# State-space turns dealt at 0.8 per attention step for the first ten, at 1.25 afterwards

## The chip, the cores and the metric

The kernel runs on one core of one Trainium2 chip. What counts is the time on the device, in microseconds (us), as a median of several runs. One execution is recorded by the hardware profiler; its numbers are in the profile.

## The reference

One inference step of a one-layer trunk of width 1024. A prompt of 1024 rows and 8 running streams of 16 new rows each (128 "sample" rows, with 1024 cached rows per stream) go through the same layer. Three mixers work on the normalised input, one projection merges them, then cross-attention into 256 memory rows and a SwiGLU block follow:

```python
proj = einsum('bnd,de->bne', u, p['w_in'])                  # one projection feeds all three
sq, sk, sv, fq, fk, fv, fg, z, xbc, dt = split_last(proj, IN_SIZES)
sb_o  = sb_attend(...)                                      # stick-breaking attention, 4 heads of 64
fox_o = fox_attend(...)                                     # attention with a forget gate, 4 heads of 64
y, h_final = ssd_scan(xs * dt[..., None], dt * A, Bm, Cm, h0, ssd_chunk)   # state space, 8 heads of 64, state 128
y = y + p['d_skip'][:, None] * xs
ssd_o = rmsnorm(y * silu(z), p['ssd_norm_g'])
h = h + einsum('bne,ed->bnd', concatenate([sb_o, fox_o, ssd_o], -1), p['w_out'])
h = h + cross_attend(rmsnorm(h, g_x), mk, mv, wq_x, wo_x)
h = h + swiglu(rmsnorm(h, g_ffn), w_gate, w_up, w_down)
```

The new keys, values, forget gates, and the state-space states after the step (`p_ssm`, `s_ssm`) are outputs too.

## The kernel before, in words

**Engines.** TensorE (PE) multiplies and transposes, VectorE (DVE) and ScalarE (ACT) work on its results, GpSimd (POOL) does elementwise work, and SyncE (SP) issues the DMAs from one queue. Each takes its instructions in the order that was fixed when the program was built. A scheduler makes that order: it is given the instructions in the order of the Python code, and follows a plan of its own of when each would be ready. So the order of the code decides much, but not all.

**Attention steps.** `pipeline` yields once per row block and once per weighted sum, over 16 prompt units and 4 sample units for each of the two attention kinds, 112 steps in all. It is the outer loop of the stretch that matters here.

**Turns.** After each step the loop at L1328 adds a rate to `acc`, and for every whole turn in `acc` it lets the generator `fill` go on by one yield. `fill_all` first runs `dense` (`fill_s`, the remaining parts of the first projection, 68 turns) and then `ssd` (`ssd_gen`, 51 turns). `RATE[0]` holds while `dense` runs, `RATE[1]` afterwards. What is left of `fill` when the attention steps are over is woven into the output projection by `weave(fill, ho, WV, "ho")` behind the loop. `hp` has no entry for these turns and changes nothing.

**State-space turns.** `ssd_gen` first sets up the decays, then goes through nine blocks in the order 8, 0, 1, ..., 7. Block 8 is the 128 sample rows, blocks 0 to 7 are 128 prompt rows each. For each block:
- `load` fetches a tile A with three DMAs: L1055 from `xbcsc`, L1057 from `acsc`, L1059 from `zsc`. These tiles, the tiles B and two tiles `st8` with the decode states come from one pool of large tiles (`act` in the rows).
- `prepare` transposes A on PE (L1072, L1076); ACT copies the results into B (L1073, L1077).
- `weights` makes the decays: PE L1087, ACT L1095 and L1100 on A, DVE L1097, L1103.
- `states` for blocks 0 to 7 is two small groups of matmuls (L1112, L1118). For block 8 it updates the states of eight streams: PE transposes L1147, ACT copies L1149, PE L1150 and L1157, DVE L1162, and at the end of each half one DMA of the new states, L1164, `s_ssm<-act`. There are two of them, and each frees one `st8` tile when it has landed.
- `outputs` is PE L1174, DVE L1176, ACT L1179, DVE L1181; `write` is PE L1186, ACT L1187 and the DMA L1188 to `mixsc`.

**Others in the rows.** L573, L574, L576 are score matmuls of the prompt, L591 to L617 its weighted sums, L900 to L908 load and transpose cached keys, L942, L943 and L951 are the sample rows' weighted sums (transposes on PE, their copies on ACT, the sums on PE). `add_rows` (L1352, residual adds on DVE) and `load_rows` (L1402 to L1416) belong to the output projection; L341 to L343 are its matmuls.

Of the kernel before, what the change touches and what calls it, by code (L numbers as in the profile page):

```python
# [51 lines left out]
XS, XH = 1, 2  # L52
X0, X1, XL = 2, 2, 2
REV = ()
RATE = (1.0, 1.1, 60)
C_SQ, C_SK, C_SV, C_FQ, C_FK, C_FV, C_Z, C_XBC, C_DT = 0, 256, 512, 768, 1024, 1280, 1540, 2052, 3076


# [5 lines left out]
def tile_hybrid_step(ctx: ExitStack, tc: tile.TileContext, a: dict):  # L64
# [307 lines left out]
    def hp(k):  # L372
        return tc.high_priority(HP[k]) if HP.get(k) else nullcontext()
# [268 lines left out]
    def pipeline(units, lag, units1, lag1):  # L642

        prev = []
        for rows, av in units + units1:
            if (rows, av) == units1[0]:
                lag = lag1
            w = []
            for f in rows:
                with hp("row"):  # L650
                    w.append(f())
                yield
            prev.append((av, w))
            if len(prev) > lag:
                f, w = prev.pop(0)
                with hp("av"):
                    f(w)
                yield
        for f, w in prev:
            with hp("av"):  # L660
                f(w)
            yield
# [590 lines left out]
    def fill_s():  # L1253
        yield from dense_T(w_in, uc, [(C_FQ, consume_qk(4, 0, QS))])
        yield from dense_T(w_in, uc, [(C_FQ + P, consume_qk(5, 1, QS))])
        yield from dense_T(w_in, uc, [(C_FK, consume_qk(6, 0, None, p_k[1], s_k[1]))])
        yield from dense_T(w_in, uc, [(C_FK + P, consume_qk(7, 1, None, p_k[1], s_k[1]))])
        for n, _ in enumerate(proj_v(1, C_FV, p_v[1], s_v[1], extra=4)):
            if n == 6:
                head = w_unit(z_srcs(0), 0, 4)  # L1260
            yield
        zs, sums = z_proj(0, head), fox_sums()
        for _ in range(4):
            next(sums)
            yield
            next(zs)
            yield
        sct = load_pads()
        for n, _ in enumerate(zs):
            if n == 2:  # L1270
                pad_cols(sct)
            yield
        for o in ORD:
            if o == "z1":

                for hd in range(4):
                    tc.keep_in_program_order(
                        SP.dma_start(out=fs4.rearrange("(b h) i k -> b h i k", h=4)[:, hd],
                                     in_=fs_sc[hd].unsqueeze(1).to_broadcast([DEC_B, 4, PAST])))
                for p in range(4):  # L1280
                    tc.keep_in_program_order(
                        SP.dma_start(out=fqs[:, p:p + 1], in_=fn_sc[8 * p:8 * p + 8, :]))
            if o[0] == "z":
                yield from z_proj(int(o[1]))
            elif o == "dt":
                dt_softplus()
                yield
            else:
                yield from xbc_proj(*o)

    def mixed(m, at, fc, nxt):


        heads = [prompt_units(m, h, fc) for h in range(4)]
        loads = [load for _, load in heads[1:]] + [nxt]
        out = []
        for h, (units, _) in enumerate(heads):
            for i, (rows, av) in enumerate(units):
                if i == 3 and loads[h]:
                    rows = [lambda f=rows[0], load=loads[h]: (load(), f())[1]] + rows[1:]  # L1300
                out.append((rows, av))
        for i, u in reversed(list(enumerate(decode_units(m)))):
            out.insert(at[i], u)
        return out, heads[0][1]
# [10 lines left out]
    u0, _ = mixed(0, AT0, None, load1)  # L1315

    dense = fill_s()
    ssd = ssd_gen()
    done = [False]

    def fill_all():
        yield from dense
        done[0] = True
        yield from ssd

    fill = fill_all()
    acc = 0.0
    for k, _ in enumerate(pipeline(u0, LAG0, u1, LAG1)):  # L1328
        acc += RATE[1] if done[0] else RATE[0]
        while acc >= 1.0:  # L1330
            with hp("ssd" if done[0] else "dense"):
                next(fill, None)
            acc -= 1.0

# [743 lines left out]
    for c in range(NCH):  # L2078
        acc = [[banks[(6 * c + 2 * i + j) % 8]() for j in range(2)] for i in range(3)]
# [63 lines left out]
```

## Time and profile before

| | us |
|---|---|
| Runs | 1865.41, 1867.77, 1865.81 |
| Median | 1865.81 |
| Profiled execution, whole | 1868.44 |
| Its span | 1866.7 |
| PE busy | 1809.8 (97%) |
| DVE, ACT, POOL busy | 897.2, 796.8, 618.6 |
| Mean granted clock of PE | 0.988 of full |

The span runs from the first to the last instruction of the profiled execution; 1.7 us lie around it. PE is the fullest engine. A gap between two of its instructions has a releaser: the instruction or DMA that ended last before PE went on. "Granted clock" is the speed at which PE was let run, 1.00 or 0.50 in the stretch that matters; PE counts as busy at half clock too.

### The profile page before, as it was taken

Reading aid. Unit: us, or ns where it says so; the run is one execution under the profiler, and the core shown is the slowest. Engines: PE = TensorE matmul, PEld = TensorE weight load, DVE = VectorE, ACT = ScalarE, POOL = GpSimd, SP = SyncE. Lnnn points to the kernel's source line nnn. Section 1 sums busy time; section 2 is a strip of 40 time slices with the busy share of each in tenths; the row PEclk is TensorE's granted clock in tenths of the full one; section 3 lists DMA queues with packets and bytes.
Section 4 is the critical chain, followed back from the end, with each engine's and each line's share of the span. In section 5 each row is a group of like instructions: output and inputs, shape, how many; then the busy total and the mean of one; then the engine's idle time right before and its main releaser. Section 6 shows DMA issues by size and latency. Waiting matters only on the chain.

```text
span 1866.7 us, 32065 instructions
## 1 busy us (share of the span) xinstructions
PE 1809.8 (97%) x12008; PEld 1620.3 (87%) x12008; DVE 897.2 (48%) x1792; ACT 796.8 (43%) x1697; POOL 618.6 (33%) x921
## 2 busy tenths in 40 slices
PE   7999999999999999999999989999999999999998
PEld 5899788888967777899988889999999999888886
DVE  3412324465646874454553695333333334455554
ACT  6532544535446772343342464333333333344443
POOL 7622434525215663121021107444444542000000
PEclk9999999999988999999999989999999999999999
DMA  9465654527577883356873124332222223656572
GB/s 338 153 186 150 211 153 132 171 79 209 179 222 253 279 278 125 118 136 155 188 252 111 68 87 116 94 79 71 72 71 71 71 71 94 217 186 238 185 242 92
DMA packets 305548, 289.55 MB, mean 155 GB/s; under 512 B 113004, under 2 KB 257364, under 8 KB 305392
## 3 DMA queue, kind: packets, MB, share of 16 engines
q1 hardware_dynamic: 305392, 287.49, 51.0%
q8 instruction: 95, 1.56, 0.4%
q14 instruction: 61, 0.50, 0.1%
HBM read 221.58 MB, written 66.38 MB: 154 GB/s over the span
## 4 chain that ended last, share of the span: by engine, by line
PE 83%; DMA 7%; DVE 4%; POOL 2%; ACT 1%; issue 1%; SPq 0%; DVEq 0%; POOLq 0%; ACTq 0%
PE psd L1936 11%; PE psd L343 10%; PE psd L341 10%; PE psd L342 10%; PE pst L1936 8%; PE pss L341 4%; PE pss L343 4%; PE pss L342 4%; PE pss L1936 4%; PE pso L1936 2%; PE pst L343 2%; PE pst L342 2%; PE pst L341 2%; PE pso L606 2%; PE pst L591 1%
## 5 line engine op out<-in xcount | busy, mean ns | idle before, releaser
L341 PE MATMUL psd<-act,wh 128*128 128x384 f32 x528 | 183.0, 347 | 1.6 <-ACT xc L761 1.6
L343 PE MATMUL psd<-act,wl 128*128 128x384 f32 x528 | 180.7, 343 | 0.7 <-POOL wl L133 0.7
L133 POOL TENSOR_TENSOR wl<-wr,wh 128x256 fp32r<-128x256 f32 (+2 forms) x152 | 117.7, 809 | 192.0 <-ACT wh L295 185.2
L342 PE MATMUL psd<-act,wh 128*128 128x384 f32 x528 | 180.3, 342 | 0.0
L1936 PE MATMUL pst<-bT,tr 128*128 128x256 f32 (+1 forms) x1068 | 154.7, 292 | 0.0
L1936 PEld LDWEIGHTS pst<-bT,tr 128*128 128x128 f32 x1068 | 144.6, 188 | 0.1
L341 PE MATMUL psd<-wh,act 128*128 128x256 f32 (+3 forms) x414 | 131.6, 322 | 3.6 <-ACT act L1415 1.5
L343 PE MATMUL psd<-wh,act 128*128 128x512 f32 (+3 forms) x424 | 135.0, 320 | 0.0
L342 PE MATMUL psd<-wl,act 128*128 128x256 f32 (+3 forms) x414 | 132.5, 321 | 2.4 <-POOL wl L133 2.3
L1936 PE MATMUL psd<-bT,tr 128*128 128x320 f32 (+1 forms) x912 | 132.6, 294 | 0.7 <-POOL tr L133 0.7
L1936 PEld LDWEIGHTS psd<-bT,tr 128*128 128x128 f32 x912 | 124.5, 188 | 1.0 <-POOL tr L133 1.0
L133 POOL TENSOR_TENSOR tr<-u,tr 128x256 fp32r<-128x256 f32 x110 | 82.8, 780 | 100.6 <-ACT tr L1772 82.8
L133 POOL TENSOR_TENSOR ws<-ws 128x256 f32<-128x256 f32 (+2 forms) x100 | 72.8, 757 | 111.5 <-DVE ws L535 91.4
L256 POOL TENSOR_SCALAR sm<-sm 128x1 f32<-128x1 f32 (+2 forms) x27 | 9.3, 343 | 295.0 <-ACT y L2047 206.6
L1911 DVE TENSOR_TENSOR tr<-tr,pst 128x256 f32<-128x256 f32 (+1 forms) x86 | 38.6, 449 | 139.3 <-ACT tr L1908 106.2
L341 PEld LDWEIGHTS psd<-act,wh 128*128 128x128 f32 x528 | 99.9, 189 | 3.6 <-ACT xc L761 2.0
L343 PEld LDWEIGHTS psd<-act,wl 128*128 128x128 f32 x528 | 99.8, 189 | 3.2 <-issue 1.9
L342 PEld LDWEIGHTS psd<-act,wh 128*128 128x128 f32 x528 | 100.0, 189 | 2.9 <-issue 2.6
L133 POOL TENSOR_TENSOR tr<-raw,tr 128x256 fp32r<-128x256 f32 x94 | 69.4, 765 | 83.4 <-ACT tr L1772 75.3
L1772 ACT CAST tr<-u 128x512 fp32r<-128x512 f32 x130 | 76.5, 620 | 27.9 <-PE pst L1936 5.9
L341 PEld LDWEIGHTS psd<-wh,act 128*128 128x128 f32 x414 | 78.3, 189 | 10.6 <-issue 1.9
L342 PEld LDWEIGHTS psd<-wl,act 128*128 128x128 f32 x414 | 78.1, 189 | 10.4 <-POOL wl L133 4.2
(645 smaller groups left out, 4645.9 us busy)
## 6 DMA issues: line engine op xcount, KB each, us to landing
u<-w_down SPq DMA_DIRECT2D x40, 512.0 KB, 3.3
raw<-w_down SPq DMA_DIRECT2D x26, 512.0 KB
st<-qksc SPq DMA_DIRECT2D x48, 256.0 KB, 5.2
wr<-w_in SPq DMA_DIRECT2D x44, 256.0 KB, 3.2
tr<-hidsc SPq DMA_DIRECT2D x55, 192.0 KB, 3.3
hidsc<-tr SPq DMA_DIRECT2D x34, 288.0 KB
qksc<-sg SPq DMA_DIRECT2D x48, 192.0 KB, 2.9
wr<-cache_sb_k SPq DMA_DIRECT2D x32, 256.0 KB, 3.0
```

Of the source, the lines that this page charges most:

```text
L133: POOL.tensor_tensor(out=out[:, a0:a1], in0=in0[:, a0:a1], in1=in1[:, a0:a1], op=op)
L256: POOL.tensor_scalar(v, ss, inv, EPS, ALU.mult, ALU.add)
L341: PE.matmul(out, ah, bh, start=start, stop=False)
L342: PE.matmul(out, ah, bl, start=False, stop=False)
L343: PE.matmul(out, al, bh, start=False, stop=stop)
L591: PE.transpose(tp[:, o:o + P], w[:, (2 * kp + j) * P:(2 * kp + j + 1) * P], ident)
L606: return PE.matmul(po[r:r + 64, q_], vt[:, 2 * (k0 + i) + j, :], pfs[i][:, sl], start=start and k0 == 0 and (j == 0 or qp > 0), stop=k0 + ...
L1772: ACT.copy(hi, src)
L1911: DVE.tensor_tensor(out=at(out, g), in0=at(x, g), in1=ps[g][:, :GW[g]], op=op)
L1936: PE.matmul(dst[g][:, :GW[g]], x[:, ka], y[:, k, :], start=start and k == 0 and m == 0, stop=stop and k == 3 and m == 2, skip_group_check= ...
```

## The change

A rate of 0.8 holds for the first ten yields of `ssd_gen`, then 1.25 to the end of the attention steps. Before, it was 1.1 throughout. 44 attention steps remain when `dense` is through, so about 48 of the 51 turns were dealt before and about 49 are now; the rest goes to `weave`. The same instructions are issued, and on every engine the order is the same up to the first state-space blocks and again from the output projection on. Between them, PE instructions 3250 to 4055 of the program stand in another order.

```diff
--- before.py
+++ after.py
@@ -52,7 +52,7 @@
 XS, XH = 1, 2
 X0, X1, XL = 2, 2, 2
 REV = ()
-RATE = (1.0, 1.1, 60)
+RATE = (1.0, 0.8, 1.25)
 C_SQ, C_SK, C_SV, C_FQ, C_FK, C_FV, C_Z, C_XBC, C_DT = 0, 256, 512, 768, 1024, 1280, 1540, 2052, 3076
 
 
@@ -1316,19 +1316,22 @@
 
     dense = fill_s()
     ssd = ssd_gen()
-    done = [False]
+    part = [0]
 
     def fill_all():
         yield from dense
-        done[0] = True
-        yield from ssd
+        part[0] = 1
+        for n, _ in enumerate(ssd):
+            yield
+            if n == 9:
+                part[0] = 2
 
     fill = fill_all()
     acc = 0.0
     for k, _ in enumerate(pipeline(u0, LAG0, u1, LAG1)):
-        acc += RATE[1] if done[0] else RATE[0]
+        acc += RATE[part[0]]
         while acc >= 1.0:
-            with hp("ssd" if done[0] else "dense"):
+            with hp("ssd" if part[0] else "dense"):
                 next(fill, None)
             acc -= 1.0
```

(Lines behind L1316 are three higher after the change: L1352 becomes L1355, L1402 L1405, L1416 L1419.)

ACT around the sample rows' first weighted sum. Before; `act_5772` is the tile that L951 reads, `act_6022` holds block 8's decays:

```order
518 L614 COPY so_6088<-pso_99 64x256
519 L1149 COPY sg_6165<-pst_6160 128x512
520 L1149 COPY sg_6172<-pst_6167 128x512
521 L1095 ACTIVATE act_6022<-act_6022,act_5975 128x128 x3
522 L1100 ACTIVATE act_6022<-act_6022 128x384
523 L943 COPY act_5772<-pst_6178 128x512
524 L1100 ACTIVATE act_6022<-act_6022 128x640
525 L943 COPY act_5772<-pst_6184 128x512
526 L555 ACTIVATE ws_6277,sm_6278<-ws_6277,sm_6278 128x640
527 L943 COPY act_5772<-pst_6190 128x128
```

After, where the decays' tile is `act_6061`:

```order
518 L614 COPY so_6057<-pso_99 64x256
519 L943 COPY act_5772<-pst_6160 128x512
520 L943 COPY act_5772<-pst_6166 128x512
521 L1095 ACTIVATE act_6061<-act_6061,act_5975 128x128 x3
522 L943 COPY act_5772<-pst_6172 128x128
523 L1100 ACTIVATE act_6061<-act_6061 128x384
524 L1100 ACTIVATE act_6061<-act_6061 128x640
525 L555 ACTIVATE ws_6244,sm_6245<-ws_6244,sm_6245 128x640
526 L1149 COPY sg_6231<-pst_6226 128x512
527 L555 ACTIVATE ws_6259,sm_6260<-ws_6259,sm_6260 128x768
```

Two L943 moved ahead of L1095, the third directly behind it, and the L1149 behind both.

PE behind those copies. Before, from the end of the block-8 transposes:

```order
2626 L1157 MATMUL psd<-act 128x256
2627 L951 MATMUL pso<-pt,act 32x128 x4
2628 L951 MATMUL pso<-vr,act 32x128 x32
2629 L1157 MATMUL psd<-act 128x256
2630 L573 MATMUL pss<-st 128x512
2631 L574 MATMUL pss<-st 128x512
2632 L573 MATMUL pss<-st 128x384
2633 L574 MATMUL pss<-st 128x384
2634 L576 MATMUL pss<-mask_fx,identr 128x128
2635 L974 MATMUL pst<-fold_156,so 128x64
2636 L1157 MATMUL pst<-act 128x256 x2
2637 L1157 MATMUL psd<-act 128x256
```

After:

```order
2620 L951 MATMUL pso<-pt,act 32x128 x4
2621 L951 MATMUL pso<-vr,act 32x128 x32
2622 L573 MATMUL pss<-st 128x256
2623 L574 MATMUL pss<-st 128x256
2624 L576 MATMUL pss<-mask_fx,identr 128x128
2625 L573 MATMUL pss<-st 128x512
2626 L574 MATMUL pss<-st 128x512
2627 L974 MATMUL pst<-fold_156,so 128x64
2628 L1147 MATMUL pst<-identr,act 128x128 x8
2629 L573 MATMUL pss<-st 128x384
2630 L574 MATMUL pss<-st 128x384
2631 L576 MATMUL pss<-mask_fx,identr 128x128
```

L951 now stands earlier, ahead of eight of the transposes L1147, and the first L1157 behind it come later.

ACT at the first prompt chunk's copies. Before, with the semaphores that each waits for:

```order
545 L1073 COPY act_6433<-psd_6434 128x512 [waits DMAHW3_49,DMAHW0_49,DMAHW4_49,PE_49,Pool_49]
546 L594 COPY pt_6483<-pst_6478 128x512 [waits PE_49]
547 L594 COPY pt_6489<-pst_6485 128x384 [waits PE_49]
548 L1077 COPY act_6433<-psd_6440 128x256 [waits PE_49]
549 L908 COPY kf_6532<-pst_6533 128x2x256 [waits PE_49]
```

After:

```order
549 L614 COPY so_6447<-pso_99 64x256 [waits DMAHW3_49,PE_49]
550 L908 COPY kf_6485<-pst_6486 128x2x256 [waits PE_49]
551 L908 COPY kf_6485<-pst_6492 128x2x256 [waits PE_49]
552 L1073 COPY act_6586<-psd_6587 128x512 [waits DMAHW1_49,DMAHW0_49,DMAHW2_49,DVE_49,Pool_49]
553 L1077 COPY act_6586<-psd_6593 128x256
554 L908 COPY kf_6508<-pst_6509 128x2x256 [waits PE_49]
```

The destination of L1073 is chunk 0's tile B in both. After the change it waits for `DMAHW1`.

SP at the second write of states. Before:

```order
441 L1164 DMA s_ssm<-act_6028 128x16x128 [waits DMAHW1_49,DVE_49]
442 L900 DMA wr_6568<-cache_fox_k 128x512 [waits DMAHW2_49,PE_49]
443 L900 DMA wr_6570<-cache_fox_k 128x512 [waits DMAHW3_49,PE_49]
444 L619 DMA mixsc_197<-so_6495 64x256 [waits DMAHW4_49,DVE_49]
445 L1055 DMA act_6450<-xbcsc_196 128x8x128 [waits DMAHW5_49,DMAHW1_49,Pool_49]
446 L1057 DMA act_6450<-acsc_203 128x1024 [waits DMAHW6_49]
```

After:

```order
441 L1164 DMA s_ssm<-act_6067 128x16x128 [waits DMAHW1_49,DVE_49]
442 L900 DMA wr_6504<-cache_fox_k 128x512 [waits DMAHW2_49,PE_49]
443 L900 DMA wr_6506<-cache_fox_k 128x512 [waits DMAHW3_49,PE_49]
444 L900 DMA wr_6521<-cache_fox_k 128x512 [waits DMAHW4_49,PE_49]
445 L619 DMA mixsc_197<-so_6447 64x256 [waits DMAHW5_49,DVE_49]
```

`DMAHW0` to `DMAHW7` are counted up in turn by SP's DMAs, and `s_ssm` here counts up `DMAHW1`. Before, the load L1055 of chunk 1 (`act_6450`) waits for it; after, ACT's L1073 above does.

DVE at the end of the state-space turns. Before; `sg_8080` is block 7's output:

```order
714 L1352 TENSOR_TENSOR st_7666<-st_7666,psd_8201 128x512
715 L1416 TENSOR_TENSOR act_8328<-act_8328 128x768
716 L1352 TENSOR_TENSOR st_8119<-st_8119,pss_8208 128x512
717 L1416 TENSOR_TENSOR act_8328<-act_8328 128x768
718 L260 SCALAR_TENSOR_TENSOR sm_8194<-sm_8193,sm_8192 128x1
719 L1403 TENSOR_TENSOR ws_8104<-ws_8104,ws_8103 128x128
720 L1403 TENSOR_TENSOR act_8112<-act_8112,ws_8111 128x128
721 L1352 TENSOR_TENSOR st_8123<-st_8123,pss_8243 128x512
722 L1181 SCALAR_TENSOR_TENSOR sg_8080<-sg_8080,sm_8194,act_5975 128x512
```

After:

```order
706 L260 SCALAR_TENSOR_TENSOR sm_8194<-sm_8193,sm_8192 128x1
707 L1181 SCALAR_TENSOR_TENSOR sg_8080<-sg_8080,sm_8194,act_5975 128x512
708 L970 SCALAR_TENSOR_TENSOR so_8057<-pso_99,frs_210,hb_163 128x128
709 L976 COPY so_8061<-pst_8059 128x64
710 L1406 TENSOR_TENSOR act_8112<-act_8112,ws_8111 128x1024
711 L1419 TENSOR_TENSOR act_8327<-act_8327 128x768 x2
712 L1355 TENSOR_TENSOR st_7662<-st_7662,psd_8155 128x512
713 L1355 TENSOR_TENSOR st_7664<-st_7664,pss_8162 128x512
```

L1181 moved ahead of the residual adds (L1352, now L1355) and the splits (L1416, now L1419).

## The prediction

> **What bounds the kernel now.** I began with the head of the profile's page: which engine is full, and whether anything else ends last.
>
> ```profile
> span 1866.7 us, 32065 instructions
> PE 1809.8 (97%) x12008; PEld 1620.3 (87%) x12008; DVE 897.2 (48%) x1792; ACT 796.8 (43%) x1697; POOL 618.6 (33%) x921
> ...
> PE 83%; DMA 7%; DVE 4%; POOL 2%; ACT 1%; issue 1%; SPq 0%; DVEq 0%; POOLq 0%; ACTq 0%
> ```
>
> TensorE (PE) is busy for 1809.8 of 1866.7 us and carries 83% of the chain that ended last. A re-dealing of turns removes no instruction, so there are two things it can win or lose: the 56.9 us in which PE stands still, and the clock that PE is granted. The change deals the state-space turns, and the two orders differ from about 535 us on, so I cut the stretch from there into pieces at the points where the granted clock changes:
>
> ```profile
> 535.40:542.15 6.75, 6.75 (x46) 4.51 (x45) 4.53 (x18) 3.97 (x10) 1.52 (x3) 1.00 0.69 195
> 542.15:545.56 3.41, 1.88 (x44) 1.40 (x46) 2.65 (x10) 2.25 (x6) 0.00 (x0) 1.00 0.11 28
> 545.56:562.63 17.07, 17.07 (x83) 11.84 (x76) 9.12 (x34) 6.29 (x13) 0.00 (x0) 0.50 0.51 143
> 579.20:582.35 3.15, 0.89 (x11) 0.66 (x7) 0.12 (x1) 0.66 (x2) 1.37 (x3) 1.00 0.96 344
> 583.11:589.94 6.83, 6.83 (x34) 6.83 (x34) 4.78 (x10) 4.02 (x9) 4.15 (x7) 0.50 1.00 364
> 589.94:666.00 76.06, 74.50 (x668) 58.79 (x667) 60.12 (x182) 55.66 (x131) 47.23 (x75) 1.00 0.78 251
> 666.00:709.00 43.00, 38.02 (x291) 27.40 (x291) 30.57 (x63) 27.71 (x51) 28.04 (x42) 1.00 0.85 299
> 709.00:840.00 131.00, 131.00 (x681) 115.03 (x683) 60.46 (x107) 43.91 (x87) 32.56 (x49) 1.00 0.38 112
> ```
>
> The second number is the length of a piece in us; then follow the busy times of PE, its weight loads, VectorE, ScalarE and GpSimd, with counts, the granted clock, the share of the DMA engines and GB/s. Between 535 and 709 us PE loses time in two ways. It idles: 1.53 us before 545.56, 2.26 us at 579 to 582, then 1.56 us up to 666 and 4.98 us up to 709. And for 17.07 us and again for 6.83 us it runs at half clock. PE is full in both, so half of each is lost: 8.5 and 3.4 us. Each follows an idle of PE of 1.5 us or more. After 709 us PE is full for the 131 us shown, so what is won before then can be carried to the end.
>
> The order of the two programs is the same on every engine outside the stretch that PE runs from 535.4 to about 707 us. Inside it the same instructions stand in another order, and the pool of large tiles gives some of them other buffers. Three places matter.
>
> **Place 1, the first stall and the long half clock.** The waits of PE from 540 to 583 us, with their total, count and longest, and the chain up to the first of them:
>
> ```profile
> PE psd L1072 <- DMA act<-xbcsc: 1.7, 1, 1.7
> PE pso L951 <- ACT act L943: 1.5, 1, 1.5
> ```
>
> ```profile
> 531.87 4.33 DMA acsc<-so
> 536.21 4.06 DMA act<-acsc
> 540.29 1.00 ACT act L1095 x3
> ...
> 544.24 0.17 ACT act L943
> 544.45 1.55 PE pso L951 x43
> ```
>
> ScalarE (ACT) takes its instructions in order. The three copies of L943, which PE's L951 needs, stand behind an L1095 that waits until 540.29 for a load; the last of them ends only when L951 starts, at 544.45. So PE idles for 1.5 us (1.48 in the trace). After the change two of the three copies stand ahead of L1095 and the third directly behind it, so L951 can start at about 541.5. But PE's own queue is shorter as well: eight transposes of L1147, an L1157, four L1150 and one pair of score matmuls now stand behind L951. By the groups of two of these in the 45 us before, at full clock,
>
> ```profile
> L1147 PE MATMUL pst<-identr,act 128*128 128x128 f32 x16 | 2.5, 280 | 0.0
> ...
> L1157 PE MATMUL psd<-act 32*128 32x256 f32 x4 | 1.4, 419 | 0.0
> ```
>
> the transposes cost 16 in 2.5 us, so eight about 1.25 us, and the L1157 0.35 us; with the scores and L1150, taken at the same pace, some 3.5 us moves behind. PE, which came at 542.97 before, then arrives at about 539.5 and idles some 2.0 us: 0.5 us worse, and again enough for the clock to drop. I take -0.5 us (between +0.5, if PE arrives a microsecond later, and -1.5).
>
> What gains is the length of the half clock. Before, L951 is followed by weak work (L1157 uses 32 of 128 rows, and 14 of these stand in the next windows), and it took five steps of 3.41 us (17.07 / 5) to end. After, L951 is followed by whole-array score matmuls and the eight transposes before the first L1157. I take two steps, 6.83 us, the length of the other one in the table: 8.5 - 3.4 = +5.1 us. The bounds: nothing if it lasts five steps again, +8.5 if the clock does not drop at all.
>
> [...]
>
> **Place 2, chunk 0.** Two writes of the decode states leave from the state tiles; the second one is the one that counts.
>
> ```profile
> 567.95 0.21 PE pst L1157
> 568.21 1.62 DVE act L1162 x6
> 569.86 6.29 DMA s_ssm<-act
> 576.21 4.63 DMA act<-xbcsc
> 580.97 0.64 PE psd L1072 x4
> 581.69 0.59 ACT act L1073
> 582.33 2.99 PE psd L1174 x16
> ```
>
> Before, chunk 1's A tile takes the buffer that this write frees. So its load starts at 576.21, and PE waits for it: 1.7 us, then about 0.5 us for the copy of L1073, 2.26 us by the piece of 579.20 to 582.35, and two steps of half clock follow. After, chunk 1's A tile has another buffer, and the tile that takes the one freed by the second write is chunk 0's B tile. Its first writer is ACT's L1073, which therefore waits for the write to land. Behind it queue all later ACT work (the copies L908 and L594, L1095) and PE's L1174 of chunk 0.
>
> Counted from the end of the last L1157 (568.16 before): the six L1162 end 1.65 us later, the write lands 6.3 us after that, L1073 takes 0.6, so L1174 starts at +8.6 (before, with the load in between, it started 14.2 us behind). PE's work between, in the new order: 7 of L591 and 16 of L906, 6 of L1072/L1076 (0.64 / 4 each), 4 of L606 and 4 of L891.
>
> ```profile
> 527.97 0.57 PE pso L606 x3
> 528.54 1.14 PE pst L591 x9
> ...
> 677.16 1.00 PE pss L891 x8
> ```
>
> That is 23 x 0.127 + 0.96 + 0.76 + 0.5 = 5.1 us. So PE stands for about 3.5 us where it stood for 2.26 before: -1.25 us. The bounds come from the nearest rows of a write: at 4.33 us (the acsc write above) the stall is 1.5 us, +0.75; if what queued behind the write delays it by another load's 4.63 us, the stall is 8.1, -5.9. I take the write's own row. The half clock that follows holds the L1174 before and after; it costs two steps in both orders, 0.
>
> The old wait for the load costs nothing now: chunk 1's L1072 stands 62 PE instructions behind that L1174, and its load no longer waits for the write. If that cover is gone, it is the same 1.7 us again.
>
> **Place 3, the end.** The last state-space block and the first output matmuls, a wait of PE and the chain's end there:
>
> ```profile
> PE psd L1186 <- DVE st L1352: 1.3, 1, 1.3
> ```
>
> ```profile
> 704.90 1.83 DVE act L1416 x2
> ...
> 706.79 0.61 DVE st L1352
> 707.45 0.66 PE psd L1186 x4
> ```
>
> Block 7's L1181 stood on VectorE (DVE) behind L1416 and several residual adds of L1352, which wait for loads and matmuls, so PE's L1186 stood 1.3 us, until 707.45. After, the L1181 stands ahead of all of them. I take +1.3 us; the bounds are 0 (the adds then make PE wait at the next matmul) and 1.3. The other idle of 589.94 to 709, 6.54 - 1.3 = 5.2 us, is dealt anew. Chunks follow each other closer at first and at the old distance later; I give -0.5 us, with 2 us on either side.
>
> **The sum.** -0.5 + 5.1 - 1.25 + 1.3 - 0.5 = 4.15 us saved. The profiled execution took 1868.44 us, its span 1866.7 and 1.7 around it, and lies 2.6 us above the median of the runs, 1865.81. Against its own time the sum gives 1864.3; the same saving from the median gives **1861.7 us**.
>
> **The rivals.**
> - *No gain at place 1.* The half clock lasts five steps whatever follows. For it: both stretches of half clock begin with small matmuls, and later L1157 still come every few instructions. Against: the shorter one ended although L1174, of 64 columns, stood in it. Place 1 gives -0.5, the rest the same: -0.95, so 1866.8 us, no change that can be told.
> [...]
> - *Slower: the wait of L1073 decides.* ACT is blocked by a write, and everything behind it is late: the copies that free PE's transposes, then the next chunks. [...] For it: the DMA share is 0.96 to 1.00 from 579 to 590, and the write shares the queue with the loads of L900. Against: the write took its 6.29 us before, with loads of 256 and 512 KB around it. [...]
> - *The change does nothing.* What is won before 709 us is lost again in a later wait, or the turns that move only shift the idle. Against: PE is full for 131 us after, and 8.5 us of half clock is too much to hide. This ends near 1865.8.
>
> **Numbers.** A change under about 0.2%, 3.7 us, cannot be told from none here. My forecast has 0.42, no gain at place 1 or no effect 0.27, no drop at place 1 0.11, the slow one 0.20. Between the ends of the costs at places 2 and 3 (about 3 us either way) the forecast falls on both sides of 1862.1; so faster takes two thirds of its chance and the 0.11, and a little of the rest: 0.42. Same is 0.38, slower 0.20. The likeliest case's own range is 1858.5 to 1865. The range that holds 8 in 10 reaches from below the case without a drop to the slow one: 1856.5 to 1871.
>
> **What the new profile would show.** Right: L951 starting near 541.5; PEclk back at 1.00 by about 552; ACT's L1073 of chunk 0 waiting for s_ssm, with a PE gap of some 3.5 us ahead of L1174 around 570; no wait of L1072 for xbcsc of chunk 1; no gap ahead of block 7's L1186. Wrong: half clock through the whole of the state updates again, a write that takes 10 us, or new gaps above 2 us between 590 and 707. [...]

## The result, and the profile after

| kernel | median of runs, us | lowest to highest, us | against before |
|---|---|---|---|
| before | 1865.61 (8 runs) | 1858.95 to 1875.89 | |
| changed | 1882.59 (8 runs) | 1876.77 to 1891.59 | 1.0085 [1.0056, 1.0114] |
| before, second comparison | 1870.47 (33 runs) | 1862.67 to 1878.95 | |
| changed, second comparison | 1883.44 (10 runs) | 1871.15 to 1891.54 | 1.0056 [1.0025, 1.0086] |

The last column is a ratio estimated from the runs, with its 95% interval; it need not be the quotient of the two medians. The change makes the kernel slower, by 10 to 16 us by the two ratios (5 to 21 us by their intervals). The forecast was 1861.7, in a range up to 1871.

The head of the profile's page of the changed kernel (its profiled execution took 1891.59 us):

```profile
span 1889.9 us, 32062 instructions
PE 1817.2 (96%) x12008; PEld 1626.9 (86%) x12008; DVE 908.3 (48%) x1792; ACT 796.0 (42%) x1697; POOL 614.0 (32%) x921
...
PE 81%; DMA 7%; DVE 4%; POOL 3%; issue 2%; ACT 1%; SPq 1%; DVEq 0%; POOLq 0%; ACTq 0%
```

The span grew by 23.2 us, PE's busy time by only 7.4: most of the loss is PE standing still. Not all of the 23 us is the change. Both traces hold 12008 matmuls, and ahead of the change and behind it PE's order is the same, so the two can be laid side by side by count. Counted from 0, the order differs from matmul 3573 to 4736. Ahead of the changed stretch (matmul 3550, at 532.31 us before and 545.02 after) the changed kernel was already 12.7 us late, 8 of it by 66 us, where one wait of PE took 6.1 us instead of 0.5 and 6.83 us of half clock came with it. That is chance: in a second profile of the changed kernel the same matmul came at 539.83, in a second profile of before at 538.17.

The stretch itself falls into three pieces: up to matmul 3925 (block 8 and chunk 0: places 1 and 2 of the prediction), from there to the first output matmul (chunks 1 to 7, which I call the middle), and the first output matmuls up to matmul 5200. One row for each piece, columns as in the prediction. Before, then before in its second profile:

```profile
532.31:593.26 60.95, 57.16 (x377) 41.36 (x376) 38.82 (x117) 31.27 (x70) 20.89 (x37) 0.80 0.74 230
593.26:684.10 90.84, 87.03 (x754) 68.00 (x752) 72.92 (x215) 68.67 (x157) 59.93 (x96) 1.00 0.80 264
684.10:785.18 101.08, 98.35 (x527) 79.42 (x525) 43.76 (x73) 32.44 (x57) 33.28 (x47) 1.00 0.42 144
```
```profile
538.17:595.78 57.61, 51.53 (x378) 37.48 (x376) 38.44 (x117) 30.90 (x70) 20.87 (x37) 0.91 0.79 240
595.78:686.31 90.53, 86.78 (x753) 68.02 (x752) 72.80 (x215) 68.67 (x157) 60.13 (x96) 1.00 0.81 268
686.31:789.26 102.95, 99.92 (x526) 80.58 (x525) 43.57 (x73) 32.44 (x57) 33.31 (x47) 0.98 0.41 141
```

The changed kernel, first and second profile:

```profile
545.02:602.49 57.47, 51.02 (x377) 36.80 (x376) 33.30 (x113) 31.23 (x70) 15.15 (x29) 0.88 0.76 224
602.49:705.81 103.32, 92.39 (x752) 71.66 (x750) 79.83 (x219) 68.04 (x158) 64.97 (x106) 0.93 0.76 248
705.81:808.94 103.13, 99.95 (x530) 80.95 (x529) 47.26 (x74) 32.54 (x57) 34.05 (x45) 0.98 0.41 137
```
```profile
539.83:595.49 55.66, 52.69 (x378) 35.72 (x376) 33.56 (x113) 31.34 (x70) 15.99 (x29) 0.85 0.75 226
595.49:697.18 101.69, 90.05 (x752) 71.15 (x750) 79.45 (x219) 67.56 (x158) 64.47 (x105) 0.97 0.77 252
697.18:800.54 103.36, 100.03 (x530) 80.98 (x528) 46.02 (x73) 32.82 (x57) 34.15 (x47) 0.98 0.41 138
```

The first piece became 2.7 us shorter on average (59.3 to 56.6), the last 1.2 us longer (102.0 to 103.2). The middle went from 90.7 to 102.5: 11.8 us. In the middle PE idled 3.8 us before (90.84 - 87.03) at full clock, and 10.9 and 11.6 us after: 7.5 us more on average. Half clock cost it another 6.8 and 3.4 us there (half of 13.7 and 6.8 us), 5.1 on average, before nothing. PE's longest waits there, before and after:

```profile
PE psd L1112 <- ACT sg L1187: 1.4, 1, 1.4
PE pst L591 <- DVE ws L560: 0.8, 1, 0.8
PE psd L1076 <- DVE sm L553: 0.4, 1, 0.4
```
```profile
PE pst L906 <- DMA wr<-cache_fox_k: 3.1, 1, 3.1
PE pss L573 <- DVE sm L548: 2.5, 2, 1.7
PE psd L1087 <- ACT sg L1187: 1.7, 1, 1.7
PE psd L1112 <- DVE act L1089: 1.4, 1, 1.4
PE pss L891 <- DVE sm L548: 1.3, 1, 1.3
```

No single wait replaces another. There are five of more than a microsecond where there was one, and they end with a DMA, with DVE and with ACT. They are no accident of one execution: the second profile of the changed kernel has the same five at the same matmuls, of 1.3 to 2.7 us.

### The profile page after: what moved, and what is told of

The parts are those of the page before. It is cut to its first block, busy times and chain, and to the rows that moved or that the text cites. A ratio compares the mean times of both kernels' runs of the same rounds, so it can differ in the third digit from the quotient of the medians.

```text
span 1889.9 us, 32062 instructions
## 1 busy us (share of the span) xinstructions
PE 1817.2 (96%) x12008; PEld 1626.9 (86%) x12008; DVE 908.3 (48%) x1792; ACT 796.0 (42%) x1697; POOL 614.0 (32%) x921
## 3 DMA queue, kind: packets, MB, share of 16 engines
q8 instruction: 95, 1.56, 0.3%
## 4 chain that ended last, share of the span: by engine, by line
PE 81%; DMA 7%; DVE 4%; POOL 3%; issue 2%; ACT 1%; SPq 1%; DVEq 0%; POOLq 0%; ACTq 0%
PE psd L1939 11%; PE psd L343 9%; PE psd L341 9%; PE psd L342 9%; PE pst L1939 8%; PE pss L341 4%; PE pss L342 4%; PE pss L343 4%; PE pss L1939 4%; PE pso L1939 2%; PE pst L341 2%; PE pst L342 2%; PE pst L343 2%; PE pso L606 2%; POOL wl L133 1%
## 5 line engine op out<-in xcount | busy, mean ns | idle before, releaser
L133 POOL TENSOR_TENSOR tr<-u,tr 128x256 fp32r<-128x256 f32 x110 | 81.9, 771 | 102.0 <-ACT tr L1775 84.3
```

The lines of the kernel that those rows point to most:

```text
L133: POOL.tensor_tensor(out=out[:, a0:a1], in0=in0[:, a0:a1], in1=in1[:, a0:a1], op=op)
```

## The experiments

I read each run in two ways: by its time against the runs of before on the same chip, and by its profile, where I count what PE lost in the three pieces: idle time, and half of the time at half clock. A run's time scatters by some 8 to 10 us either way, so the profile says more on where, the interval more on how much.

**1. Which half of the change.** The table of rates alone was edited, in the changed kernel's code:

```diff
-RATE = (1.0, 0.8, 1.25)
+RATE = (1.0, 0.8, 1.1)     # r1: first part only
+RATE = (1.0, 1.1, 1.25)    # r2: second part only
```

> Only the first part of the change: 0.8 for the first ten turns, then the old 1.1. PE's order is that of the changed kernel up to the third chunk, then another one. Theory A (the loss comes from chunks 1 to 7 being dealt closer at 1.25): this keeps the gain of about 4 us at the first two places and loses little afterwards, so 1860 to 1866 us against 1865 before. Theory B (the slow start is to blame: chunk 1 comes late, its loads bunch up on SP's queue and every later chunk waits): this loses as much as the whole change, 1876 to 1884 us.

> Only the second part: 1.1 for the first ten turns, then 1.25. PE's order is that of before up to the fourth chunk. Theory A: it loses 10 us or more, 1875 to 1885 us, with the half clock of before at the state updates kept. Theory B: it stays within 3 us of before, 1863 to 1868 us.

Measured: the first part alone 1.0008 [0.9987, 1.0029], the second alone 1.0015 [0.9994, 1.0037]. Neither is the whole loss, and neither theory's numbers fit: A wanted 10 us from the second part, B as much from the first. Whether each costs nothing or a part is not settled: their medians, 1875.55 and 1876.15 us, lie 5.1 and 5.7 us above the 1870.47 of before, and the intervals allow up to 5 and 7 us. The middle of each:

```profile
585.17:676.79 91.62, 82.66 (x717) 65.18 (x715) 75.47 (x211) 67.14 (x155) 59.25 (x95) 0.98 0.79 261
```
```profile
597.02:694.19 97.17, 89.77 (x765) 70.57 (x764) 74.62 (x219) 67.47 (x156) 63.33 (x104) 0.98 0.76 249
```

With the first part alone PE idles 9.0 us there, with the second alone 7.4, before 3.8. In its profile the first part alone made it good elsewhere: its first piece took 53.7 us. That execution, of 1866.65 us, was the fastest of its 12 runs. (The middle holds somewhat different work in each build, 717 to 765 matmuls, so idle times are compared and not lengths.)

**2. The same kernel again, and the loads on another queue.** r3 is the changed kernel unaltered. In r4 the loads of tile A are issued by GpSimd:

```diff
-            SP.dma_start(out=A[:, 0:1024]...      # and the two below
+            POOL.dma_start(out=A[:, 0:1024]...
```

> The changed kernel once more, unaltered, for a second profile. In its first profile the instructions ahead of the change, the same in both kernels, ended 12 us later than in the profile of before, and the changed stretch itself took 11.3 us more. If the first is chance and the second is the change, the second profile has the changed stretch 9 to 14 us longer again (from the first L942 that moved to the first output matmuls), and the part ahead of it anywhere between 0 and 12 us later. Time 1877 to 1886 us.

> The changed kernel with the three loads of each chunk's tile A issued by GpSimd instead of SP, so that they do not stand behind SP's other transfers. If the lateness of these loads on SP's queue (two chunks' loads issued back to back at 612 to 616 us, the last landing 8.9 us later) is what costs the time, most of the 11 us comes back: 1866 to 1874 us. If the waits come from elsewhere, or from the DMA engines being full, it stays at 1878 to 1886; GpSimd's own work can be delayed by a load that waits for its buffer, which would make it worse still.

r3: 1.0056 [1.0025, 1.0086], the stretch 8 us longer than in the first profile of before (260.7 against 252.9 up to matmul 5200), a little less than forecast, and ahead of it 7.5 us late instead of 12.7. r4: 1.0064 [1.0040, 1.0087], middle idle 11.4 us. Taking the loads off SP's queue gave no time back, although the waits of ACT and DVE for the load `acsc` (experiment 4) fell from 16.1 to 6.9 us.

**3. Slower and faster second rates.**

```diff
+RATE = (1.0, 0.8, 1.0)     # r5
+RATE = (1.0, 0.8, 0.8)     # r6
+RATE = (1.0, 1.1, 0.9)     # r7
+RATE = (1.0, 0.8, 1.6)     # r8
```

> 0.8 for the first ten turns, then 1.0: the chunks are dealt a fifth slower than in the changed kernel (1.25), a tenth slower than with 1.1 after 0.8. The changed stretch took 252.9 us of PE's time before, 251.5 with 0.8 / 1.1, 263.9 and 260.7 with 0.8 / 1.25. Theory A (the loss is the density of the chunks: each comes before its loads, copies and decays are through): slower dealing leaves fewer waits, so the stretch takes 246 to 251 us, the run 1862 to 1868 beside a before of about 1868. Theory C (which of PE's waits meet is a matter of the order that each build happens to get, not of density): anywhere between 250 and 262.

> 0.8 throughout. Some 14 of the turns are left over when the attention steps end and go between the output projection's steps. Theory A: the attention part has fewest waits of all (stretch up to the output projection shorter by another few us), but the last chunks meet the output projection, whose matmuls fill PE; together 246 to 252 us if they hide there. Theory C: 250 to 262 as above.

> 1.1 for the first ten turns as before, then 0.9. The state updates and the first prompt chunk stand as before, with their long half clock. Theory A: 247 to 252 us for the stretch. Theory C: 250 to 262.

> 0.8 for the first ten turns, then 1.6, denser still than the changed kernel. Theory A: more and longer waits of PE than at 1.25: stretch 266 to 275 us, run 1885 or more. Theory C: 250 to 264, not longer than at 1.25.

Measured: 1.0094 [1.0062, 1.0127], 1.0113 [1.0091, 1.0135], 1.0073 [1.0043, 1.0103], 1.0099 [1.0068, 1.0131]. All are slower, so theory A's forecast that slower dealing saves time falls. What slower dealing costs shows in the last piece. For r6 (0.8 throughout):

```profile
673.31:807.03 133.72, 118.47 (x622) 94.94 (x621) 58.71 (x94) 41.33 (x78) 49.89 (x72) 0.96 0.41 136
```
```profile
PE psd L341 <- ACT ws L1405: 4.2, 2, 2.6
```

The turns left over meet the output projection: PE idles 15.2 us in that piece instead of 2.7, waiting for the splits (4.2 us in this row) and residual adds. With 1.0 it was 9.5 us, with 0.9 10.4. So there is a floor under the rate. But in the middle all builds that start at 0.8 for ten turns idle 8.3 us or more, whatever follows (8.6 at 0.8, 8.3 at 1.0, 9.0 at 1.1, 12.5 at 1.6), and the build with 1.1 and 0.9 only 3.9.

Density is not cleared by this, though. Side by side, the middle's idle of builds that start at 1.1 is 3.9, 4.3, 3.8, 3.8 and 7.4 us for second rates of 0.9, 1.05, 1.1, 1.15 and 1.25 (1.05 and 1.15 are r12 and r11 below). Of those that start at 0.8 it is 8.6, 8.3, 9.0, 11.3 and 12.5 for 0.8, 1.0, 1.1, 1.25 and 1.6. So by this count the slow start adds 4 to 5 us of idle at either of the second rates that both rows share, and 1.25 in place of 1.1 adds 2 to 4 more: both halves of the change cost something in the middle. Most of these are one profile each.

**4. The decays' load, and the neighbours of before.** ACT and DVE wait in the middle for one load, `acsc` (L1057). After and before:

```profile
ACT act L1095 <- DMA act<-acsc: 12.6, 4, 7.9
DVE act L1097 <- DMA act<-acsc: 3.5, 5, 1.5
```
```profile
ACT act L1095 <- DMA act<-acsc: 4.0, 3, 2.0
DVE act L1097 <- DMA act<-acsc: 2.8, 2, 1.6
```

r9 and r10 cut it to an eighth, in the changed kernel and in before (the decays of seven of eight heads are left out); r11 and r12 step the second rate of before up and down:

```diff
-            SP.dma_start(out=A[:, 1024:2048], in_=ac_sc[8*i:8*i+8, :]...)   # 512 KB
+            SP.dma_start(out=A[:, 2560:2688], in_=ac_sc[8*i:8*i+1, :]...)   # 64 KB, r9 and r10
# r9, r10: all heads' decays are worked out from that one row (lines not shown)
+RATE = (1.0, 1.1, 1.15)    # r11
+RATE = (1.0, 1.1, 1.05)    # r12
```

> The changed kernel with the decays' load of the prompt chunks cut from eight heads (512 KB, L1057) to one head (64 KB); every instruction on PE, ACT and DVE stays, all heads read that one head's row, so the decays of seven heads are left out. PE's order is that of the changed kernel but for small shifts. Between the first prompt chunk and the output projection PE lost (idle, plus half of the half-clock time) 19.5 and 15.1 us in the two profiles of the changed kernel, and 9.5 us before. ACT and DVE wait there for this load for 16 us, before for 7. Theory D (the late decay load blocks ACT and DVE, and the attention rows behind it make PE wait): the loss falls to 11 us or less, the run to 1866 to 1874 beside a before of 1868. Theory C (the waits come from the order as such, on all engines): 14 us or more stay, the run is at 1876 to 1884.

> The same cut of the decays' load in the kernel before, as the counterpart. Theory D: it had few waits for this load, so it gains 1 to 3 us only (loss 7 to 9 us in that stretch, run 1865 to 1868). Theory C: within 3 us of before either way, since the order hardly changes.

> 1.1 for the first ten turns, then 1.15: one step from before on the dense side; PE's order is that of before up to the sixth chunk. Theory A (density): between before and 1.1 / 1.25, which lost 6 us more between the first chunk and the projection: 1 to 3 us slower than before. Theory C (each build's order meets its waits by chance, and before is one of the luckier ones): anywhere from 2 us faster to 10 us slower, with no link to the size of the step.

> 1.1 for the first ten turns, then 1.05: one step on the other side. Theory A: 1 to 3 us less lost among the chunks, and a little more in the projection, where 0.9 lost 9 us: about even with before. Theory C: anywhere from 2 us faster to 10 us slower.

r9: 1.0078 [1.0046, 1.0109], no better. The waits for the load were as long with 64 KB (its lines stand five lower):

```profile
ACT act L1100 <- DMA act<-acsc: 15.5, 5, 6.9
DVE act L1102 <- DMA act<-acsc: 6.9, 5, 3.1
```

So cutting its size did not bring it earlier. But an eighth of the bytes did not make the load itself much shorter: of the loads that stand in the chains, three took 5.0 to 8.9 us at 512 KB in the changed kernel, and two took 4.8 and 4.9 us at 64 KB in r9. First the changed kernel, then r9:

```profile
615.15 8.92 DMA act<-acsc
669.04 5.01 DMA act<-acsc
```
```profile
607.01 4.94 DMA act<-acsc
631.65 4.83 DMA act<-acsc
```

So r9 tests a smaller load, and hardly a quicker one. r10: 1.0032 [1.0015, 1.0049]; instead of the forecast gain it lost 3 to 9 us. r11: 1.0014 [0.9985, 1.0042], r12: 1.0017 [0.9997, 1.0036], middle idle 3.8 and 4.3 us: the neighbours of before are as good as before. Before is no lucky single point.

**5. Before again, and relieving one queue.** In r14 the loads of the attention stacks go by GpSimd; in r15 two more heads' decays go from DVE to ACT; in r16 the products with the decays go from DVE to GpSimd:

```diff
-            SP.dma_start(out=f32(t[0:64, :]), ...      # load_stacks, all three loads
+            POOL.dma_start(out=f32(t[0:64, :]), ...    # r14
-NACT = 3
+NACT = 5                                               # r15
-FSC, CBE = "D", "DD"
+FSC, CBE = "D", "PP"                                   # r16
```

> The kernel before once more, unaltered, for a second profile. If its one profile was typical, PE's changed stretch takes 250 to 255 us again (252.9 in the first), with 8 to 11 us lost between the first prompt chunk and the projection. If it was a lucky one, it takes 257 or more, and the difference to the changed kernel is smaller than the profiles say.

> The changed kernel with the loads of the attention stacks (L520, L521, L523) issued by GpSimd. On SP the first of them waits 7.9 us for a buffer, and the loads of the next chunks and of cached keys stand behind it. Theory F (SP's blocked queue makes the loads late): the waits of PE for xbcsc, acsc and cached keys go, 3 to 6 us come back, run 1870 to 1876. Theory C (the order as such): the stretch stays at 258 us or more, run 1877 or more.

> The changed kernel with two more heads' decays moved from DVE (L1097) to ACT (L1095), NACT 5 instead of 3. About 6 of the 11 us that PE idles among the chunks end with a DVE instruction (L548, L970, L1406, L1089). Theory E (DVE's in-order queue is what comes late): the waits for DVE shrink, the stretch falls to 252 to 257 us, run 1868 to 1876. Theory C: 258 us or more; other waits, of ACT above all, take their place.

> The changed kernel with the products of the decays (L1103, two of 512 columns in each chunk, 0.7 to 1.1 us each) moved from DVE to GpSimd. Theory E: as in the run with five heads, 252 to 257 us for the stretch. Theory C, or GpSimd in turn too late: 258 us or more.

r13 gave 251.1 us for the stretch, 252.9 the first time: typical. r14: 1.0070 [1.0049, 1.0090], r15: 1.0070 [1.0047, 1.0094], r16: 1.0089 [1.0063, 1.0115], with 14.4, 11.2 and 13.4 us idle in the middle. None of the reliefs brought the time back, so relieving one of these queues alone is not enough. In r14, where nothing of the attention stacks stood ahead of the chunk loads, the wait for one of them was even the longest of all:

```profile
PE psd L1072 <- DMA act<-xbcsc: 6.3, 2, 5.4
```

By then the builds fell into two groups. Where chunk 1's transposes stood late in PE's order (matmuls 3918 to 3931 instead of 3852 to 3856), PE waited 1.5 to 5.4 us in all right ahead of chunk 2's transposes, at matmuls 4062 to 4067, in every profile. Where chunk 1 stood at its old place, there was no such wait in any. In the changed kernel the transposes L1072 of chunk 1 are matmul 3928 instead of 3852 and those of chunk 2 are 4067 instead of 3979; chunk 3 comes at 4151 instead of 4116, chunk 4 at 4233 instead of 4222, chunk 5 at its old place. In time chunk 2 followed chunk 1 by 19.6 us before (48.7 to 68.3 us behind the start of the stretch) and by 14.2 us after (57.8 to 72.0), 2.0 of them waits. In matmuls the distance grew, from 127 to 139; before, 6.83 us of the interval ran at half clock. A short interval alone is not enough, though: before, chunk 3 follows chunk 2 by 12.4 us with a wait of 0.2. What else has to meet there can be seen on DVE in the changed kernel, where PE's L573 waits for the first L548:

```profile
610.83 1.71 DVE L1103 TENSOR_TENSOR act<-act 128x512 f32<-128x512 f32 x2
612.46 0.68 DVE L1114 TENSOR_TENSOR sg<-psd,act 128x512 f32<-128x512 f32 x1
613.84 0.67 DVE L258 SCALAR_TENSOR_TENSOR sm<-sm 128x1 f32<-128x1 f32 x1 [0.70 <-POOL sm L257]
...
615.30 0.68 DVE L548 CUSTOM_DVE_ANT_0 ws<-pss,xc 128x512 f32<-128x512 f32 x1
```
```profile
616.05 0.33 PE L573 MATMUL pss<-st 128*128 128x128 f32 x1 [1.69 <-DVE sm L548]
...
616.98 1.08 PE L1072 MATMUL psd<-identr,act 128*128 128x128 f32 x4 [0.34 <-DMA act<-xbcsc]
```

L548, the attention's own work, stands behind chunk 1's decays and states (L1103, L1114) and behind the norm of the chunk ahead (L258 to L260), which waits for GpSimd. In r1, r4, r6, r14 and r16 the wait ends with the load of chunk 2 instead. So the place is common to all builds with a late chunk 1; what arrives last there is not.

**6. One turn more or less.** This pair tests that. Both keep the changed order at the first weighted sum; only the number of slow turns differs.

```diff
-RATE = (1.0, 0.8, 1.25)
+RATE = (1.0, 0.8, 1.1)
-            if n == 9:
+            if n == 4:         # r17; n == 5 in r18
```

> 0.8 for the first five turns only, then 1.1. PE's order at the first weighted sum (L951) and through block 8 is that of the changed kernel, but chunk 1's transposes L1072 stand at row 2675 of PE's order, where they stood before, not at 2699. In all profiles with chunk 1 late (2697 to 2700, all eight builds that start at 0.8 for ten turns) PE idles 8 to 14 us between the chunk-0 block and the projection, with 1.5 to 5.4 us of it right ahead of chunk 2; in the six builds with chunk 1 at 2675 to 2678 it idles 3.8 to 7.4 there. Theory B (the late chunk 1, with chunk 2 close behind it, is the cause): 3.5 to 7 us idle in that stretch, no wait above 1 us ahead of chunk 2, and the run at or below before (1860 to 1868 where before has 1866). Theory C (any other order than before's is as bad): 8 us or more idle, 1872 or more.

> The same with one turn more: 0.8 for the first six turns, then 1.1. Chunk 1's L1072 now stand at row 2702 and chunk 2's at 2717. Theory B: the wait ahead of chunk 2 is back (1.5 us or more), 8 us or more idle in that stretch, and the run slower than with five turns by 3 to 10 us. Theory C: no link between the two.

With five slow turns chunk 1 stands at its old place: 1.0015 [0.9988, 1.0041], 1870.34 us beside 1869.25. With six it is late: 1.0056 [1.0035, 1.0077], 1879.14 us. One turn costs 0.4% (1.0056 less 1.0015), 8.8 us between the medians of 12 runs each. The middle of the two, idle 6.5 and 7.9 us, and PE's longest waits in it:

```profile
589.58:683.23 93.65, 87.17 (x742) 68.59 (x742) 71.32 (x214) 67.54 (x157) 61.02 (x95) 0.96 0.75 258
```
```profile
PE psd L1087 <- DVE sg L1176: 4.9, 2, 3.0
```
```profile
587.61:680.74 93.13, 85.19 (x738) 65.85 (x737) 77.41 (x211) 67.20 (x156) 62.50 (x99) 1.00 0.79 264
```
```profile
PE pss L573 <- DVE sm L548: 2.5, 3, 1.5
PE pst L591 <- ACT pt L594: 1.9, 1, 1.9
```

The wait ahead of chunk 2 (L573 for L548, 1.5 us, then 0.5 for the load) is there with six turns and not with five. Theory B holds in its direction and in the difference of the two; r17 was not faster than before, as B would have allowed, but even, and the 7.9 us of idle in r18 are just short of B's 8. What the two profiles do not show is where the 8.8 us lie. The profiled execution of r18 was the fastest of its 12 runs, 1871.5 us, and up to matmul 5200 the stretch took 254.2 us in r17 and 254.0 in r18. Nor does the one turn move chunk 1 alone: in the first piece PE waits 2.05 us for cached keys (L906) with five, and 1.54 us for L1073, as at place 2, with six. So the pair shows that the sixth slow turn costs 0.4%, and that the wait ahead of chunk 2 comes with it; that this wait, or the late chunk 1, is what costs it is likely and not shown.

All builds by chunk 1's place:

| chunk 1 | builds | idle of PE in the middle, us | against before |
|---|---|---|---|
| in time | before (two profiles), 1.1/1.25, 1.1/1.15, 1.1/1.05, 0.8 for five turns | 3.8, 3.8, 7.4, 3.8, 4.3, 6.5 | 1, 1, 1.0015, 1.0014, 1.0017, 1.0015 |
| in time, other costs | 1.1/0.9 (turns left over), before with short load | 3.9, 6.7 | 1.0073, 1.0032 |
| late | 0.8/1.25 (two profiles), 0.8/1.6, 0.8 for six turns | 10.9, 11.6, 12.5, 7.9 | 1.0085, 1.0056, 1.0099, 1.0056 |
| late, other costs | 0.8/1.0, 0.8/0.8 (turns left over) | 8.3, 8.6 | 1.0094, 1.0113 |
| late, 0.8/1.25 with one thing relieved | r4, r9, r14, r15, r16 | 11.4, 14.1, 14.4, 11.2, 13.4 | 1.0064, 1.0078, 1.0070, 1.0070, 1.0089 |
| late, and even by its interval | 0.8/1.1 for ten turns (r1) | 9.0 | 1.0008 |

r1 is the exception. It pays in the middle like the others, with 3.0 us ahead of chunk 2, and its first piece is 4 to 7 us shorter than that of before. Whether that is its order or the clock's luck there is open: its one profile is of its fastest run, and its median lies 5.1 us above that of before. No build beat before.

## Why the prediction was wrong

**Place 1: right in the order of the copies, its gain resting on one execution.** The two copies moved as forecast, and L951 started directly behind the third:

```profile
553.77 0.99 ACT act L1095 x3
554.75 0.16 ACT act L943
...
554.96 3.87 PE pso L951 x72
```

PE's idle ahead of it was 2.34 us in one profile and 1.12 in the other (forecast 2.0). The half clock was to shrink from 17.1 to 6.8 us, +5.1. In the first profile it did, to 3.4 and again 3.4 after a second wait. In the second one the 1.12 us did not bring the clock down at all; it fell later, behind a wait of 0.90 us inside the state updates, and stayed at half for 17.1 us, one of the prediction's signs of being wrong:

```profile
558.38 0.45 PE L1157 MATMUL psd<-act 32*128 32x256 f32 x1 [0.90 <-DVE act L1162]
```

And before, unaltered, had only 3.4 us of half clock at L951 in its second profile:

```profile
551.17:554.58 3.41, 3.27 (x64) 3.05 (x68) 2.09 (x9) 1.12 (x3) 0.00 (x0) 0.50 0.00 0
```

So the 17 us that the sum was built on belonged to an execution, not to the order. Five further builds have the same PE order here (r2, r7, r10, r11, r12), and all seven profiles have the same wait ahead of L951, 1.48 or 1.49 us. In four of them the half clock began between 0.14 us ahead of L951's start and 0.76 us behind it, and lasted 3.41 us; in three it began 0.95 to 1.12 us behind it, and lasted 17.07 us. Places 1 and 2 together gained 2.7 us on average (forecast -0.5 + 5.1 - 1.25 = 3.35), a size that agrees by chance.

**Place 2: right in the mechanism, in the first profile near in size.** The second write took 5.84 us, ACT's L1073 waited for it, and L1174 followed:

```profile
579.35 5.84 DMA s_ssm<-act
...
586.00 3.67 PE psd L1174 x16
```

(L1174 here is the output of block 8, which shares PE's result buffers with chunk 0's transposes. The prediction took it for chunk 0's; block 8's own stood at 570.45 before, and chunk 0's, with which it was compared, at 582.33.) PE idled 0.82 + 1.56 = 2.4 us there (forecast 3.5, before 2.26), and the old wait of chunk 1 for its load was gone from the first profile. In the second profile ACT's L1073 waited for the write too, but only 0.59 us, PE's L1174 did not wait, and PE idled the 0.82 us alone; chunk 1's wait for its load was 0.95 us there.

**Place 3: right for L1186, whose wait fell from 1.33 to 0.1 us, but not for its sum.** A wait of 1.73 us for L970 ahead of L974 took its place, and the last piece is 1.2 us longer instead of 1.3 shorter.

**The step that failed is the one with the least working: "the other idle ... is dealt anew", -0.5 us with 2 us on either side.** The middle measured -11.8 us: 7.5 us more idle and 5.1 us lost to half clock, for which the sum had no term there, with slightly less work of PE against it. I had read from the order that the chunks follow each other closer at first and at the old distance later, and I priced that by the idle of before. But the idle of before belonged to the old distances. With chunks 1 and 2 some 80 matmuls later and chunk 5 in its old place, which stood in the order, chunks 3 and 4 follow by 84 and 82 matmuls instead of 137 and 106. Other attention rows then meet each chunk's copies, decays and norm in the in-order queues of ACT, DVE and GpSimd, and the -0.5 had no row behind it. The waits are shown; that this meeting is what makes them is argued, from the rows of the one ahead of chunk 2. The sixth slow turn costs about 0.4% (r17 and r18), and the table goes with a late chunk 1 but for r1; why each of the five waits of the changed kernel arises was not taken apart further and stays open.

**The rivals.** The slower case was named, but with another cause: the wait of L1073 for a write that lands late. The write took 5.8 us, and 6.29 before. The two ends of the range, from a case without a drop of the clock at place 1 (chance 0.11) and from the slow one (0.20), were estimates of mine that no run shows: in the changed kernel's first profile the clock dropped at L951 behind 2.34 us of idle, in the second it fell only later, and for 17.1 us. The range ended at 1871, and the profiles put the loss where no rival had a price. One of the prediction's signs of being wrong did point there: new gaps above 2 us between 590 and 707 (the longest is 3.1 us, for cached keys).

## What to carry to other kernels

When a change re-deals side work, list its units by their place in the busiest engine's order before and after: where units move against the main work, waits of several engines can appear that no row of the old profile prices, and a bound of a few us on either side is then too narrow. A stall or a slow stretch that one profile shows must be seen in a second profile of the same kernel before a gain is built on its removal. And a rate that spreads work over a loop has a floor as well: what is left over at the end is paid in the next stage.

## What the runs showed of the hardware

Half clock came behind short pauses. I cut the first profiles of before and of the changed kernel, from 70 to 1850 us, into pieces of 3413 ns counted from their changes of clock: every stretch of the record between its first and last change is a whole number of these, and half clock lasted 3.41, 6.83, 10.24 or 17.07 us. The clock dropped 4 times before and 12 times after. In the piece just ahead of a drop PE had idled 1.53 to 1.91 us before and 1.33 to 2.46 us after. In the pieces at full clock that no drop followed it had idled up to 1.47 and 1.69 us, so idles between 1.33 and 1.69 us stand on both sides. In the second profile of the changed kernel PE idled 0.90 us in the first row, among the state updates' matmuls of 32 rows, and the clock was half in the next 17 us:

```profile
556.70:560.10 3.40, 2.50 (x18) 1.45 (x16) 3.40 (x15) 2.26 (x7) 0.00 (x0) 1.00 1.04 250
560.10:577.20 17.10, 17.10 (x62) 10.24 (x63) 7.81 (x26) 5.90 (x11) 2.33 (x7) 0.50 0.57 164
```

The same wait ahead of L951, 1.48 or 1.49 us, was followed in the first profile of before by 17.07 us of half clock that began 1.11 us behind L951's start, and in the second by 3.41 us that began 0.14 us ahead of it.

Cutting a 512 KB load to 64 KB left the waits for it as long (16 and 22 us in all), and the load itself still took 4.8 to 4.9 us. Issued by GpSimd (r4) it was waited for 6.9 us instead of 16.1, so SP's queue had a share in its lateness; the time came back in neither.
